# Retention: one small VectorE instruction with two tensor inputs becomes two with one tensor input each

## The chip, the core and the metric

The kernel runs on one core of a Trainium2 chip. A core has five engines that run their own instruction streams side by side and wait for each other by semaphores: TensorE (PE in the profile; its weight loads are PEld), VectorE (DVE), ScalarE (ACT), GpSimd (POOL) and SyncE (SP), which here issues most of the DMAs. The metric is the time of one execution on the device, in microseconds; lower is better.

## The reference

The program is one step of a two-layer decoder trunk on 1024 prompt tokens and 8 single-token sequences, all in fp32. Layer 0 is multi-scale retention, layer 1 a chunked gated MLP. What matters here is the end of the retention mixer: the output of each head, 512 wide, is normalised over its width, multiplied by a gain and by the SiLU of a gate, and projected.

```python
o = jnp.moveaxis(o, 0, 1).reshape(B, L, RET_HEADS, RET_DV)
mu = jnp.mean(o, -1, keepdims=True)
var = jnp.mean(jnp.square(o - mu), -1, keepdims=True)
o = ((o - mu) * lax.rsqrt(var + LN_EPS)).reshape(B, L, RET_VW) * gn_gain.astype(jnp.float32)
y = (jax.nn.silu(g.astype(jnp.float32)) * o).astype(x.dtype) @ w_out
```

## The kernel before

Every fp32 matmul is done as three: each operand is split into a high part (rounded) and a low part (the remainder), and high x high, high x low and low x high are summed in PSUM. The splits cost ScalarE a copy and VectorE or GpSimd a subtraction of two SBUF tensors.

The order of the work is the order of the code; nothing is rescheduled. The retention stage (some 580 to 770 us in the profile) is a loop of 16 rounds, n = 4h + c, over 4 heads and 4 chunks of 256 tokens each. A chunk has two row blocks of 128 tokens (`ib`). In round n the calls are, in this order:

- `r_stat(n - 1)`: VectorE takes the mean and variance of the two row blocks of the chunk before out of PSUM (`mv`, 128x2x2), adds epsilon (`rstn`), and GpSimd raises that to the power -1/2 (`rsrn`, line 254), which gives the reciprocal deviation.
- `r_pre(n + 1)`: PE transposes the keys of the next chunk (`kt`), VectorE makes their low part (`kd`); `r_split(n + 2)` then has GpSimd subtract for the low parts `qkl` and `vl` of the chunk after that, two instructions of 128x1024 on line 495, both inputs in SBUF; `r_on(n - 1)` comes next; then the scores `sc`, masked by VectorE to `p`, and their low part `phl` by GpSimd.
- `r_state(n)`: the running state `T`, and its split `sh` (ScalarE) and `sl` (VectorE, line 555, both inputs in SBUF).
- `r_inner(n)` and `r_cross(n)`: the output `o` in PSUM.
- `r_y(n - 1)`: PE transposes `on` (line 619), VectorE multiplies by gain and gate (`yT`, line 623: one input in PSUM, one in SBUF, and a column of gains). In the rounds with n mod 4 = 1, `r_cross(n)` comes ahead of it, in all others behind it. In round 0 of a head `r_cross` does nothing.

`r_on(n)` is the function that the change touches. It applies (o - mean) x deviation as one ScalarE pass per row block, with a scale and a bias per partition. The bias is -mean x reciprocal deviation, `nb`, 128x2, which VectorE makes from `mv` and `rsrn`. So `rsrn` (GpSimd) comes before `nb` (VectorE), that before `on` (ScalarE), and that before the transposes `y` (PE). The code issues the subtractions `qkl` and `vl` on GpSimd's queue directly behind `rsrn`, except in the last two rounds, where there is no chunk left to split; GpSimd has splits of the projection's weights (line 134) there.

Of the kernel before, what the change touches and what calls it, by code (L numbers as in the profile page):

```python
# [14 lines left out]
ALU = mybir.AluOpType  # L15
# [26 lines left out]
def retnet_gmlp_step(ctx: ExitStack, tc: tile.TileContext, a, o):  # L42
    nc = tc.nc
    act, dve, pool, pe, sp = nc.scalar, nc.vector, nc.gpsimd, nc.tensor, nc.sync
# [8 lines left out]
    def S(name, shape=(128, T), dt=F32):  # L53
        return big.tile(list(shape), dt, tag="s", name=name)
# [443 lines left out]
    def r_pre(n):  # L498
        if n >= NS:
            r_on(n - 2)  # L500
            return
        r = R[n]
        ps = PS(f"kt{n}")
        for jb in range(2):
            for d in range(2):
                pe.transpose(ps[:, jb * 256 + d * 128:jb * 256 + (d + 1) * 128],
                             r["qk"][:, 2 + d, jb * 128:(jb + 1) * 128], ident)
        kd = S(f"kd{n}", (128, 2, 512), F32R)
        act.copy(kd[:, 0, :], ps)
        dve.tensor_tensor(kd[:, 1, :], ps, f(kd[:, 0, :]), ALU.subtract)  # L510
        r["kd"] = kd
        if n:
            r_split(n + 1)
        r_on(n - 2)
        sc = PS(f"sc{n}")
        hh, ll = r["qkh"], r["qkl"]
        for jb in range(2):
            for d in range(2):
                ks = slice((2 + d) * CH + jb * 128, (2 + d) * CH + (jb + 1) * 128)
                qs = slice(d * CH + jb * 128, (d + 1) * CH)  # L520
                mm3(sc[:, jb * CH:CH + jb * 128], hh[:, ks], ll[:, ks], hh[:, qs], ll[:, qs], d == 0, d == 1)
        pt = S(f"p{n}", (128, 384))
        dve.tensor_tensor(pt, sc[:, :384], RC["mask"], ALU.mult)
        phl = S(f"phl{n}", (128, 2, 384), F32R)
        act.copy(phl[:, 0, :], pt)
        pool.tensor_tensor(phl[:, 1, :], pt, f(phl[:, 0, :]), ALU.subtract)
        r["p"] = phl
# [68 lines left out]
    def r_on(n):  # L596
        if n < 0:
            return
        r = R[n]
        rs = r["rs"]  # L600
        nb = small.tile([128, 2], F32, tag="nb", name=f"nb{n}")
        dve.scalar_tensor_tensor(nb, r["mv"][:, :, 0], -1.0, rs[:, 0:2], ALU.mult, ALU.mult)
        on = S(f"on{n}", (128, 2, DV))
        for ib in range(2):
            act.activation(on[:, ib, :], r["o"][ib], AF.Identity, bias=nb[:, ib:ib + 1], scale=rs[:, ib:ib + 1])
        r["on"] = on
# [326 lines left out]
    for n in range(NS):  # L933
# [19 lines left out]
        if n == NS - 1:  # L953
# [3 lines left out]
            outb.pre_load(1)  # L957
    r_stat(NS - 1)
    r_on(NS - 1)

    def r_last(q, n, tb):
# [589 lines left out]
```

## Time and profile before

| | |
|---|---|
| median of 3 runs | 1748.51 us (1746.86 to 1751.27) |
| the profiled execution | 1749.73 us, span 1748.0 us |
| PE busy, share of the span | 1692.2 us, 97% |
| VectorE, ScalarE, GpSimd busy | 900.0, 664.9, 407.5 us |
| mean granted TensorE clock | 0.987 of full |

The span is from the first to the last instruction of the program. Matmuls are pipelined, so a busy PE is not PE at its peak. [...] In a timeline row, the brackets at the end hold the idle time of the engine just before the instruction, and what ended it.

### The profile page before, as it was taken

How to read it: one execution, taken by the hardware profiler on the slowest of the kernel's cores; microseconds unless marked ns; L12 is line 12 of the kernel's file. 1: busy time of each engine (PE TensorE's matmuls, PEld its weight loads, DVE VectorE, ACT ScalarE, POOL GpSimd, SP SyncE). 2: the span in 40 equal slices, each digit the busy share in tenths (PEclk: the TensorE clock that was granted, in tenths of full speed). 3: DMA queues.
4: the chain of work that ended last, by engine and by line, in shares of the span. 5: the costliest groups of instructions: out<-in, count | busy, mean ns of one | idle time of the engine just before them, and what ended most of it. 6: DMA issues, size and time to landing. Idle time of an engine off the chain costs nothing. (4 is left out here: it accounts for less than half of the span.)

```text
span 1748.0 us, 25438 instructions
## 1 busy us (share of the span) xinstructions
PE 1692.2 (97%) x10304; PEld 1511.5 (86%) x10304; DVE 900.0 (51%) x1446; ACT 664.9 (38%) x1043; POOL 407.5 (23%) x331
## 2 busy tenths in 40 slices
PE   9999999999999999999999999997899999999996
PEld 8898897979999887877778999996889999977775
DVE  7134453633331577753359574564465555543347
ACT  4122424234332454431205343344556666731102
POOL 4122231411110666531107100011111111231103
PEclk9999999999999999999999999998999999999998
DMA  7135555555532544341102312263655666692206
GB/s 266 72 122 191 183 204 187 212 165 209 217 145 93 197 157 157 133 181 49 49 25 110 110 73 97 84 178 78 152 147 151 157 164 157 152 324 89 82 1 171
DMA packets 103174, 248.76 MB, mean 142 GB/s; under 512 B 9264, under 2 KB 37824, under 8 KB 103056
## 3 DMA queue, kind: packets, MB, share of 16 engines
q1 hardware_dynamic: 92736, 222.78, 36.5%
q0 software_dynamic: 10112, 24.15, 7.8%
q8 instruction: 81, 1.33, 0.3%
q14 instruction: 37, 0.30, 0.0%
q10 hardware_dynamic: 208, 0.20, 0.0%
HBM read 152.83 MB, written 69.93 MB: 127 GB/s over the span
## 5 line engine op out<-in xcount | busy, mean ns | idle before, releaser
L63 PE MATMUL fm<-xl,wh 128*128 128x344 f32 x768 | 246.6, 321 | 1.2 <-DVE xl L301 0.8
L63 PE MATMUL fm<-xh,wh 128*128 128x344 f32 x768 | 246.4, 321 | 1.3 <-ACT xh L300 1.3
L63 PE MATMUL fm<-xh,wl 128*128 128x344 f32 x768 | 246.1, 320 | 0.0
L63 PE MATMUL op<-wh,yh 128*128 128x512 f32 x512 | 202.4, 395 | 0.0
L63 PE MATMUL op<-wl,yh 128*128 128x512 f32 x512 | 201.7, 394 | 0.0
L63 PE MATMUL op<-wh,yl 128*128 128x512 f32 x512 | 201.7, 394 | 0.0
L63 PEld LDWEIGHTS fm<-xh,wh 128*128 128x128 f32 x768 | 144.9, 189 | 5.6 <-ACT xh L300 2.0
L63 PEld LDWEIGHTS fm<-xl,wh 128*128 128x128 f32 x768 | 144.7, 188 | 3.0 <-DVE xl L301 1.3
L63 PEld LDWEIGHTS fm<-xh,wl 128*128 128x128 f32 x768 | 144.7, 188 | 0.0
L130 ACT CAST wh<-wr 128x1024 fp32r<-128x1024 f32 x83 | 86.0, 1047 | 143.0 <-PE pd L63 58.9
L665 DVE TENSOR_TENSOR pre<-pre,op 128x512 f32<-128x512 f32 x96 | 65.7, 684 | 141.4 <-PE op L63 141.4
L134 DVE TENSOR_TENSOR wl<-wr,wh 128x1024 fp32r<-128x1024 f32 x77 | 107.6, 1403 | 46.2 <-ACT wh L130 28.6
L412 DVE SCALAR_TENSOR_TENSOR dw<-s,qd_dec,dw 128x512 f32<-128x512 f32 x32 | 40.0, 1251 | 170.1 <-ACT dw L411 170.1
L63 PEld LDWEIGHTS op<-wh,yh 128*128 128x128 f32 x512 | 96.1, 188 | 23.8
L63 PEld LDWEIGHTS op<-wh,yl 128*128 128x128 f32 x512 | 96.1, 188 | 22.7
L63 PEld LDWEIGHTS op<-wl,yh 128*128 128x128 f32 x512 | 96.2, 188 | 22.2
L63 PE MATMUL tm<-wl,xh 128*128 128x512 f32 x256 | 101.1, 395 | 0.0
L63 PE MATMUL tm<-wh,xl 128*128 128x512 f32 x256 | 100.9, 394 | 0.0
L63 PE MATMUL tm<-wh,xh 128*128 128x512 f32 x256 | 100.9, 394 | 0.0
L420 POOL TENSOR_TENSOR dhl<-dw,dhl 128x512 fp32r<-128x512 f32 x32 | 43.3, 1353 | 242.3 <-ACT dhl L419 234.4
L355 ACT ACTIVATE v<-tm,gneg 128x512 f32<-128x512 f32 x32 | 22.0, 689 | 202.3 <-PE tm L63 184.6
L1171 POOL DMA_DIRECT2D w_p<-wr x32 | 28.6, 895 | 295.8 <-PE tm38a L63 169.6
(829 smaller groups left out, 4262.4 us busy)
## 6 DMA issues: line engine op xcount, KB each, us to landing
wr<-in_w SPq DMA_DIRECT2D x127, 512.0 KB
s<-in_state SPq DMA_DIRECT2D x32, 512.0 KB
out_rs<-s SPq DMA_DIRECT2D x32, 512.0 KB
y_s<-yy SPq DMA_DIRECT2D x17, 512.0 KB
qk_s<-ro SPq DMA_DIRECT2D x16, 512.0 KB
v_s<-v SPq DMA_DIRECT2D x16, 512.0 KB
vbc<-vd_s SPq DMA_DIRECT2D x16, 512.0 KB
g_s<-g SPq DMA_DIRECT2D x16, 512.0 KB
```

The costliest lines, as they stand in the source:

```text
L63: pe.matmul(out, lhs, rhs, start=start, stop=stop, skip_group_check=skip)
L130: act.copy(t, src)
L134: eng.tensor_tensor(t, src, f(W[p][half][0]), ALU.subtract)
L355: act.activation(t[:, i % 2, :], ps, AF.Copy, scale=gneg[:, 2 * h + i % 2:2 * h + i % 2 + 1])
L412: dve.scalar_tensor_tensor(w[:, 0, :], s[:, 0, :], qd_dec[:, h, 0, b:b + 1], w[:, 1, :], ALU.mult, ALU.add)
L420: pool.tensor_tensor(hl[:, 1, :], w, f(hl[:, 0, :]), ALU.subtract)
L665: dve.tensor_tensor(dst, dst, ps, ALU.add)
L1171: pool.dma_start(self.op[k][1], src, accum_op=ALU.add)
```

## The change

Line 602 made both columns of `nb` with one SCALAR_TENSOR_TENSOR, whose two tensor inputs are the means and the reciprocal deviations, both in SBUF. Now there is a loop over the two row blocks with one TENSOR_SCALAR each: its tensor input is the column of means (128x1), and it is multiplied by the constant -1 and by the column of reciprocal deviations, which is read as a per-partition scalar.

```diff
         nb = small.tile([128, 2], F32, tag="nb", name=f"nb{n}")
-        dve.scalar_tensor_tensor(nb, r["mv"][:, :, 0], -1.0, rs[:, 0:2], ALU.mult, ALU.mult)
+        for ib in range(2):
+            dve.tensor_scalar(nb[:, ib:ib + 1], r["mv"][:, ib, 0:1], -1.0, rs[:, ib:ib + 1], ALU.mult, ALU.mult)
         on = S(f"on{n}", (128, 2, DV))
```

VectorE's queue in round 1, where `nb` of chunk 0 is made, before (line, operation, out<-in, size, and the semaphores that the instruction waits for; the numbers behind names are buffers):

```order
L510 TENSOR_TENSOR kd_4929<-kt_4924,kd_4929 128x512 [waits Activation_49]
L602 SCALAR_TENSOR_TENSOR nb_4940<-mv_4915,rsrn_4921 128x2 [waits Pool_49]
L523 TENSOR_TENSOR p_4958<-sc_4945,mask 128x384 [waits PE_49]
L549 SCALAR_TENSOR_TENSOR T_4977<-T_4890,st_0_4963 128x512 [waits PE_49]
L549 SCALAR_TENSOR_TENSOR T_4977<-T_4890,st_1_4970 128x512 [waits PE_49]
L555 SCALAR_TENSOR_TENSOR sl_4981<-T_4977,sh_4980 128x1024 [waits Activation_49]
```

The same place with the change:

```order
L510 TENSOR_TENSOR kd_4929<-kt_4924,kd_4929 128x512 [waits Activation_49]
L603 TENSOR_SCALAR nb_4940<-mv_4915,rsrn_4921 128x1 [waits Pool_49]
L603 TENSOR_SCALAR nb_4940<-mv_4915,rsrn_4921 128x1
L523 TENSOR_TENSOR p_4959<-sc_4946,mask 128x384 [waits PE_49]
L549 SCALAR_TENSOR_TENSOR T_4978<-T_4890,st_0_4964 128x512 [waits PE_49]
L549 SCALAR_TENSOR_TENSOR T_4978<-T_4890,st_1_4971 128x512 [waits PE_49]
L555 SCALAR_TENSOR_TENSOR sl_4982<-T_4978,sh_4981 128x1024 [waits Activation_49]
```

One instruction became two in the same place, the first of which waits for GpSimd as the old one did; no other instruction of VectorE changes its place.

ScalarE's queue in the same round, before:

```order
L494 CAST vh_4936<-vv_4909 128x1024 [waits DMAHW7_49]
L605 ACTIVATE on_4942<-o_0_4897,nb_4940,rsrn_4921 128x512 [waits DVE_49]
L605 ACTIVATE on_4942<-o_1_4898,nb_4940,rsrn_4921 128x512
L525 CAST phl_4960<-p_4958 128x384 [waits DVE_49]
L554 ACTIVATE sh_4980<-T_4977 128x1024 [waits DVE_49]
```

The same with the change:

```order
L494 CAST vh_4936<-vv_4909 128x1024 [waits DMAHW7_49]
L606 ACTIVATE on_4943<-o_0_4897,nb_4940,rsrn_4921 128x512 [waits DVE_49]
L606 ACTIVATE on_4943<-o_1_4898,nb_4940,rsrn_4921 128x512 [waits DVE_49]
L525 CAST phl_4961<-p_4959 128x384 [waits DVE_49]
L554 ACTIVATE sh_4981<-T_4978 128x1024 [waits DVE_49]
```

The second half of `on` now has a wait of its own on VectorE.

## Rows read from the trace of the kernel before

**Rows 1.** The page, part 1: busy us, share of the span, instructions.
```profile
PE 1692.2 (97%) x10304; PEld 1511.5 (86%) x10304; DVE 900.0 (51%) x1446; ACT 664.9 (38%) x1043; POOL 407.5 (23%) x331
```

**Rows 2.** PE's waits, 580 to 770 us: total us, times, longest.
```profile
PE y L619 <- ACT on L605: 10.3, 12, 2.4
```

**Rows 3.** Windows, PE: stretch, length, busy (instructions), granted clock, DMA share, GB/s.
```profile
601.31:616.48 15.17, 12.41 (x60) 0.89 0.06 19
611.40:614.80 3.40, 3.40 (x12) 0.50 0.00 0
616.48:626.83 10.35, 10.35 (x58) 1.00 0.27 82
...
644.75:657.64 12.89, 10.78 (x59) 1.00 0.20 70
668.50:676.90 8.40, 8.01 (x47) 1.00 0.97 312
687.62:702.40 14.78, 12.15 (x59) 0.88 0.33 107
696.80:700.20 3.40, 3.08 (x11) 0.50 0.00 0
```

**Rows 4.** Line 602: grouped (busy us, mean ns | idle before); then ns min/median/max.
```profile
L602 DVE SCALAR_TENSOR_TENSOR nb<-mv,rsrn 128x2 f32<-128x2 f32 x16 | 22.3, 1393 | 5.1 <-POOL rsrn L254 5.1
...
L602 DVE SCALAR_TENSOR_TENSOR nb<-mv,rsrn x16: 160/2331/2391, 596.6 to 757.9; 128x2 f32<-128x2 f32 x16
```

**Rows 5.** Timeline, 607 to 612 us, round 2: start us, us, engine, instruction.
```profile
607.28 2.38 POOL L495 TENSOR_TENSOR qkl<-qk,qkh 128x1024 fp32r<-128x1024 f32 x1
607.34 2.33 DVE L602 SCALAR_TENSOR_TENSOR nb<-mv,rsrn 128x2 f32<-128x2 f32 x1 [0.20 <-POOL rsrn L254]
...
609.60 2.36 POOL L495 TENSOR_TENSOR vl<-vv,vh 128x1024 fp32r<-128x1024 f32 x1
609.76 1.45 ACT L605 ACTIVATE on<-o,nb,rsrn 128x512 f32<-128x512 f32 x2 [5.33 <-DVE nb L602]
...
610.60 0.33 PE L619 MATMUL y<-ident,on 128*128 128x128 f32 x1 [2.42 <-ACT on L605]
...
611.92 1.00 POOL L526 TENSOR_TENSOR phl<-p,phl 128x384 fp32r<-128x384 f32 x1
```

**Rows 6.** Timeline, 735 to 738 us, round 14, without splits on line 495.
```profile
735.74 0.16 DVE L602 SCALAR_TENSOR_TENSOR nb<-mv,rsrn 128x2 f32<-128x2 f32 x1 [0.21 <-POOL rsrn L254]
735.82 0.56 DVE L523 TENSOR_TENSOR p<-sc,mask 128x384 f32<-128x384 f32 x1
736.00 1.45 ACT L605 ACTIVATE on<-o,nb,rsrn 128x512 f32<-128x512 f32 x2 [4.08 <-DVE nb L602]
...
737.37 0.90 PE L619 MATMUL y<-ident,on 128*128 128x128 f32 x6
```

**Rows 7.** Timeline, 944 to 947 us, the projection behind retention.
```profile
944.43 2.39 POOL L713 TENSOR_TENSOR pre<-pre,lnb 128x1024 f32<-128x1024 f32 x1 [1.26 <-ACT pre L705]
...
945.75 0.15 DVE L251 TENSOR_SCALAR rstl<-lmv 128x1 f32<-128x1 f32 x1
```

**Rows 8.** Timeline, 1529 to 1534 us, in layer 1.
```profile
1528.90 2.41 POOL L134 TENSOR_TENSOR wl<-wr,wh 128x1024 fp32r<-128x1024 f32 x1
1529.01 2.33 DVE L1380 CAST y1d<-ydt 128x8 fp32r<-128x8 f32 x1
...
1531.37 2.28 DVE L1381 TENSOR_TENSOR y1d<-ydt,y1d 128x8 fp32r<-128x8 f32 x1
```

**Rows 9.** Timeline, 730 to 733 us.
```profile
730.62 3.40 POOL L134 TENSOR_TENSOR wl<-wr,wh 128x1024 fp32r<-128x1024 f32 x1
...
731.67 1.65 DVE L623 SCALAR_TENSOR_TENSOR yT<-y,gng,gg 128x256 f32<-128x256 f32 x4
```

**Rows 10.** Timeline, 675 to 680 us, round 9.
```profile
677.42 1.45 DVE L555 SCALAR_TENSOR_TENSOR sl<-T,sh 128x1024 fp32r<-128x1024 f32 x1 [3.41 <-ACT sh L554]
677.75 2.00 POOL L526 TENSOR_TENSOR phl<-p,phl 128x384 fp32r<-128x384 f32 x1
```

## The prediction

> **What bounds the kernel now.** I read the page's busy shares first: TensorE (PE) is busy for 1692.2 of 1748.0 us [rows 1], so a change counts only where PE stands still or runs slowly. Second, PE's waits in the retention stage, 580 to 770 us: one line holds nearly all of it, the transposes of `on` waiting for ScalarE, 10.3 us in 12 waits, the longest 2.4 [rows 2]. Third, the stage cut into its rounds [rows 3]. A round of one kind (c = 1, 2 or 3 of a head) takes 10.35 us where nothing stops it; three others take 15.17, 12.89 and 14.78. [...]
>
> Fourth, the instruction that the change replaces. `nb` is 128x2, yet its 16 instances take 22.3 us, 1393 ns on average, from 160 to 2391 [rows 4]. Instances of 2.35 and of 0.16 us give 22.3 with nine long and seven short ones. The timeline shows what a long one is [rows 5]: GpSimd starts `qkl`, a subtraction with both inputs in SBUF, at 607.28; `nb` starts at 607.34 and ends at 609.67, when `qkl` ends at 609.66. It is a hold and not work. Behind it ScalarE had been idle for 5.33 us, starts `on` at 609.76, and PE starts `y` at 610.60 after 2.42 us of waiting; with the wait for the second half of `on` the round has 15.17 - 12.41 = 2.76 us of PE idle [rows 3]. In the last head the same round has no subtraction behind the power: `nb` takes 0.16 us, `on` starts 0.26 us after `nb`, and PE transposes without a wait [rows 6].
>
> **The change, part by part.** Removed: 16 instances, nine of about 2.35 us and seven of 0.16. Added: 32 TENSOR_SCALAR of 128x1. The trace has that operation and size elsewhere: 0.15 us at 945.75 [rows 7]. Behind a short `nb` the next VectorE instruction starts 0.08 us after it started (735.82 after 735.74 [rows 6]), so a second small one costs 0.08 to 0.16 and I take 0.25 for the pair. ScalarE's second half now waits for the second one alone, which is done 0.8 us before the first half of `on` is, so that wait is free.
>
> The question is whether TENSOR_SCALAR is held too. The rows say no, in two halves. At 945.75 a 128x1 TENSOR_SCALAR began 1.3 us into a GpSimd addition of 2.39 us with two SBUF inputs, and took 0.15 us [rows 7]. That one had a constant where the new one has a column of `rs` from SBUF. For that operand, `yT` has one tensor from PSUM, one from SBUF and a column from SBUF: four in a row took 1.65 us inside a GpSimd subtraction of 3.40 us [rows 9]; these are free of a hold, so a column does not bring one. What the trace lacks is both in one instruction. Bounds for a pair: 0.25 us (not held) and 4.6 us (both held, one after the other, as the 2.33 and 2.28 us at 1529.01 and 1531.37 [rows 8]). I take 0.25, since the nearest row in operation and size is not held.
>
> A held `nb` then ends 2.35 - 0.25 = 2.1 us sooner, nine times. Seven unheld ones end about 0.1 us later; of those, most stand behind ScalarE's casts, where 0.1 us does not show, so I count nothing.
>
> What PE gets of it:
> - Its waits for `on`, 10.3 us [rows 2]. One, in the round 668.50 to 676.90, follows an unheld `nb` (span less busy 8.40 - 8.01 = 0.4 us [rows 3]) and stays. That leaves 9.9 us. The three waits in c = 2 rounds (span less busy: 2.76; 12.89 - 10.78 = 2.1; 14.78 - 12.15 = 2.6 [rows 3]) are as long as the gain of 2.1 or longer, so 0.7 + 0 + 0.5 = 1.2 us would be left over by that alone. But the round before also lets VectorE finish earlier, since its `nb` is held too. I leave 0.8: gain 9.1 us.
> - The clock. With waits of at most 0.7 us in place of 2.4, I expect both stretches at 0.50 to run at 1.00. A stretch of 3.4 us at half speed holds 1.7 us of full-speed work, so each returns 1.7: gain 3.4 us. This is the 0.89 and 0.88 in the mean clock of the two rounds.
> - Restarts. Round 644.75 is 12.89 - 10.35 = 2.54 us over its undisturbed like, of which 2.11 is wait; round 601.31 is 4.82 over, of which 2.76 + 1.7 = 4.46. So some 0.4 us a stopped round goes into refilling PE; three such: 1.0 us.
>
> Sum: 9.1 + 3.4 + 1.0 = 13.5 us. What is late next? VectorE's `sl`, the other instruction here with two SBUF inputs. It now asks during `vl`, 2.1 us sooner, and is held until that ends; at 677.42 it was, then ran ahead of GpSimd's `phl`, which was drawn out to 2.00 us from 1.00 in the round of [rows 5] [rows 10]. `phl` is read a round later, so that is covered. If `phl` goes first instead, VectorE keeps its old finishing time, the 1.2 us above stay whole and a wait of 0.7 us recurs. Loads do not become the bound: they are issued as tiles come free, which moves with PE.
>
> The rest of the program has PE as its bound too, so what the stage gains reaches the end. The profiled execution took 1749.73 us (span 1748.0), 1.2 above the median of the runs, 1748.51. 1748.51 - 13.5 = 1735.0.
>
> [...] At 1529.01 a cast of 128x8, one tensor input, is held for 2.33 us behind a GpSimd subtraction [rows 8], so a single input is no safeguard. [...]
>
> **Rivals.**
> - Slower: the pair is held, twice in a row. The first part ends with `qkl`, as `nb` does now; the second then starts inside `vl`, which follows at 609.60 [rows 5], and is held for another 2.3 us, as the pair at 1529.01 was. `on` comes 2.3 us later. In six rounds PE already waits on it with `vl` behind (the three above, and three with waits of 0.2 to 0.4 in what is left of the 10.3), so 6 x 2.3 = 14 us, and one to four more clock stretches at 1.7 each: 16 to 21, say 1767. It decides as soon as the second instruction meets a GpSimd subtraction. Against it: the row at 945.75. Chance 0.07.
> - No effect: only the first is held, the second slips through between `qkl` and `vl`. 1748.5 give or take 1. `vl` starts before `nb` ends [rows 5], so there is hardly a gap. Chance 0.05.
> - Part of it given back: the hold goes, but `sl` and `phl` take turns the other way, or the clock falls elsewhere. 13.5 less 1 to 2 of leftover waits, less 3.4 of clock, less their restarts: a gain of 5 to 10, about 1740. For it: later stages have their own stretches at 0.50 which a shift by 13 us may move by one or two. Chance 0.18, of which 0.02 with under 5.2 us.
> - The forecast: all three terms, a gain of 11 to 17: 1732 to 1738. Chance 0.70.
>
> **How the numbers follow.** A measurement of this kernel tells 0.3% (5.2 us) from no change. Faster by more: 0.70 + 0.16 = 0.86. Within: 0.05 + 0.02 = 0.07. Slower: 0.07. The time is the forecast's, 1735. The range leaves out the two held cases (0.12) and a little of the small gains: below, every microsecond of the four rounds' excess plus one moved clock stretch elsewhere (18 us); above, the gain of waits without clock and with leftovers (6 us): 1730 to 1742.5.
>
> **What would show it.** Right: all 32 TENSOR_SCALAR at about 0.15 us with `qkl` running; ScalarE's idle time ended by `nb` down by some 2 us a held round; PE's waits for `on` down from 10.3 to 1 or 2 us; no clock of 0.50 between 600 and 735; the three long rounds at 10.4 to 11. Wrong: a TENSOR_SCALAR of 2.3 us, above all the second of a pair; PE's wait for `on` replaced by one for `phl` or `sl`; the stage shorter and the end not.

## The result, and the profile after

The changed kernel takes 1733.07 us (median of 4 runs, 1732.42 to 1735.48) where the one before takes 1748.34 (median of 4): ratio 0.9913, 95% interval 0.9896 to 0.9930, so 12 to 18 us faster. In a later set of runs it was 1733.88 us, ratio 0.9916, 0.9903 to 0.9930. The forecast was 1735.

The timeline of the changed kernel in round 2, the stretch that answers to [rows 5] (here and below, rows that don't bear on the reading are left out of timelines):

```profile
605.84 0.70 POOL L254 TENSOR_TENSOR rsrn<-rstn,mhalf 128x2 f32<-128x2 f32 x1 [2.39 <-DVE rstn L253]
606.51 2.42 POOL L495 TENSOR_TENSOR qkl<-qk,qkh 128x1024 fp32r<-128x1024 f32 x1
606.57 0.33 DVE L603 TENSOR_SCALAR nb<-mv,rsrn 128x1 f32<-128x1 f32 x2 [0.20 <-POOL rsrn L254]
...
606.88 1.45 ACT L606 ACTIVATE on<-o,nb,rsrn 128x512 f32<-128x512 f32 x2 [2.92 <-DVE nb L603]
...
607.72 0.33 PE L620 MATMUL y<-ident,on 128*128 128x128 f32 x1
...
608.38 0.98 PE L620 MATMUL y<-ident,on 128*128 128x128 f32 x7 [0.34 <-ACT on L606]
...
609.75 2.60 DVE L555 SCALAR_TENSOR_TENSOR sl<-T,sh 128x1024 fp32r<-128x1024 f32 x1 [1.19 <-ACT sh L554]
611.23 1.99 POOL L526 TENSOR_TENSOR phl<-p,phl 128x384 fp32r<-128x384 f32 x1
```

GpSimd's `qkl` starts at 606.51, and the pair runs beside it in 0.33 us. PE's wait of 2.42 us is gone; 0.34 for the second half of `on` is left. `sl` is now the instruction that is held (2.60 us; the shortest of its 12 instances here takes 1.23), it then runs ahead of `phl`, which takes 1.99 us, and PE waits for neither.

All 32 instances of the new instruction (ns min/median/max), and the waits of PE in the stage, 580 to 770 us:

```profile
L603 DVE TENSOR_SCALAR nb<-mv,rsrn x32: 201/210/217, 596.8 to 744.0; 128x1 f32<-128x1 f32 x32
```

```profile
PE y L620 <- ACT on L606: 0.3, 1, 0.3
PE sc L63 <- POOL qkl L495: 0.3, 1, 0.3
```

None is held, at most 217 ns each, though 11 of the 16 pairs run inside a GpSimd subtraction (9 instances, of 2.33 to 2.39 us, were held before). PE waits 0.3 us in the place of the 10.3 of [rows 2]. The rounds of the changed kernel, stretch, length, PE busy, clock, which answer to [rows 3]:

```profile
600.84:611.99 11.15, 10.80 (x60) 1.00 0.13 46
611.99:622.34 10.35, 10.35 (x59) 1.00 0.18 58
640.29:650.95 10.66, 10.56 (x59) 1.00 0.25 85
661.29:669.09 7.80, 7.79 (x47) 1.00 0.99 322
679.40:690.09 10.69, 10.57 (x59) 1.00 0.45 149
```

The three long rounds went from 15.17, 12.89 and 14.78 to 11.15, 10.66 and 10.69 us, at clock 1.00 throughout. The first projection matmul starts at 737.57 us, before at 751.65: the stage gives 14.1 us. What lies behind it is the same program in both. From that matmul to the end, in the kernel before, after, and in the second profile of the changed kernel:

```profile
751.65:1748.02 996.37, 954.97 (x6225) 0.98 0.42 121
```

```profile
737.57:1730.71 993.14, 951.42 (x6225) 0.99 0.42 122
```

```profile
737.49:1732.83 995.34, 955.22 (x6225) 0.98 0.41 122
```

The 3.2 us by which the first profile was shorter there came back in part in the second. Over the profiles of the eight experiments that leave this part alone it takes from 992.0 to 999.0 us, so the 3.2 us lie within its scatter and are not claimed for the change. At least a part of the scatter is the clock: between 760 and 1700 us the kernel before has 27.3 us at 0.50, the first profile of the changed kernel 17.1, the second 27.3 again.

### The profile page after: what moved, and what is told of

Its sections match the earlier page's. It is cut to its first block, busy times and chain, and to the rows that moved or that the text cites. A ratio compares the mean times of both kernels' runs of the same rounds, so it can differ in the third digit from the quotient of the medians.

```text
span 1730.7 us, 25453 instructions
## 1 busy us (share of the span) xinstructions
PE 1685.0 (97%) x10304; PEld 1506.6 (87%) x10304; DVE 891.3 (52%) x1462; ACT 665.0 (38%) x1043; POOL 413.5 (24%) x331
```

## The experiments

The theory: a VectorE instruction that reads two SBUF tensors is held while GpSimd runs a subtraction that reads SBUF; `nb` was such an instruction on the path to PE. Rivals: the old form is slow in itself; the split into two, or the size, is what counts and not the number of inputs; the gain comes from elsewhere in the stream. Each kernel was timed beside the one before on the same chip (1748.4 to 1749.2 us).

**1. Split, but two inputs each.**

```diff
-        dve.scalar_tensor_tensor(nb, r["mv"][:, :, 0], -1.0, rs[:, 0:2], ALU.mult, ALU.mult)
+        for ib in range(2):
+            dve.scalar_tensor_tensor(nb[:, ib:ib + 1], r["mv"][:, ib, 0:1], -1.0, rs[:, ib:ib + 1], ALU.mult, ALU.mult)
```

> nb split in two as in the change, but each half a SCALAR_TENSOR_TENSOR with both columns as tensor inputs (128x1). Theory (what holds is the second SBUF input): the first half is held by qkl, the second by vl, some 4.6 us together where it was 2.35; this is the rival of the prediction that ends on the other side: 16 to 21 us slower than before, 1764 to 1769 us. Rival (it is the size of one element a row, or the split, that frees it): as with the change, 1733 us.

Measured: 1752.24 us, ratio 1.0018 (1.0007 to 1.0029). Its timeline in round 2, and all instances:

```profile
607.03 2.37 POOL L495 TENSOR_TENSOR qkl<-qk,qkh 128x1024 fp32r<-128x1024 f32 x1
607.10 2.39 DVE L603 SCALAR_TENSOR_TENSOR nb<-mv,rsrn 128x1 f32<-128x1 f32 x2 [0.20 <-POOL rsrn L254]
609.36 2.36 POOL L495 TENSOR_TENSOR vl<-vv,vh 128x1024 fp32r<-128x1024 f32 x1
...
610.34 0.33 PE L620 MATMUL y<-ident,on 128*128 128x128 f32 x1 [2.41 <-ACT on L606]
```

```profile
L603 DVE SCALAR_TENSOR_TENSOR nb<-mv,rsrn x32: 144/156/2387, 596.4 to 760.0; 128x1 f32<-128x1 f32 x32
```

Size, number and place are those of the change, and so is ScalarE's separate wait for the second half; only the operation differs, and with it the kind of the second operand. The gain is gone. So neither the split nor the size of one element frees `nb` by itself. It is not the operation's name either: in [rows 9] the same one, with one of its tensors in PSUM, is not held (four inside the subtraction take 0.47 us each, the median of all 64). But my price for a second hold was wrong: both together took 2.39 us and not 4.6. The second instruction, queued right behind the first without a wait, gets in as `qkl` ends and `vl` starts (609.34 and 609.36). The pair at 1529.01 [rows 8] was held twice (2.33 and 2.28 us), and there the second waits for the first's result; that this difference is the cause was not tried.

**2. One input, two elements a row, made beside the power.**

```diff
+        ng = small.tile([128, 2], F32, tag="ng", name=f"ng{n}")
+        dve.tensor_scalar(ng, r["mv"][:, :, 0], -1.0, None, ALU.mult)
+        for ib in range(2):
+            dve.tensor_scalar(nb[:, ib:ib + 1], ng[:, ib:ib + 1], rs[:, ib:ib + 1], None, ALU.mult)
```

> Each instruction has one tensor input, but the first is 128x2: the means are negated in one TENSOR_SCALAR of 128x2 with a constant, then multiplied by the deviations in two of 128x1. Theory A (one tensor input is never held): as with the change, plus 0.15 us a chunk: 1733 to 1735 us, all 48 instructions at about 0.2 us. Theory B (one input is held as well when its size along the row is even, as the 128x8 cast was; one element is not): the 128x2 one is held 2.3 us in nine or more chunks, the two behind it run free: 1748 to 1752 us.

Measured: 1731.94 us, ratio 0.9913 (0.9893 to 0.9933). It reads like theory A, but the test was a poor one, as its timeline in round 1 shows:

```profile
595.84 0.73 POOL L254 TENSOR_TENSOR rsrn<-rstn,mhalf 128x2 f32<-128x2 f32 x1 [0.82 <-DVE rstn L253]
596.28 0.16 DVE L603 TENSOR_SCALAR ng<-mv 128x2 f32<-128x2 f32 x1
596.50 2.44 POOL L495 TENSOR_TENSOR qkl<-qk,qkh 128x1024 fp32r<-128x1024 f32 x1
596.61 0.34 DVE L605 TENSOR_SCALAR nb<-ng,rsrn 128x1 f32<-128x1 f32 x2 [0.17 <-POOL rsrn L254]
```

`ng` needs the means alone, so it was done before `qkl` started and never met it. It says nothing about a hold by a subtraction. It did start inside GpSimd's power `rsrn`, which reads SBUF too, in 14 of 16 chunks, and that did not hold it (0.16 us at 596.28, with the power running from 595.84 to 596.57).

**3. The same, but waiting for the power.**

```diff
+        ng = small.tile([128, 2], F32, tag="ng", name=f"ng{n}")
+        dve.tensor_scalar(ng, rs[:, 0:2], -1.0, None, ALU.mult)
+        for ib in range(2):
+            dve.tensor_scalar(nb[:, ib:ib + 1], ng[:, ib:ib + 1], r["mv"][:, ib, 0:1], None, ALU.mult)
```

> Like the experiment with one tensor input and 128x2, but now the 128x2 instruction negates the deviations, so it can only start when GpSimd's power is done, that is with qkl: it meets the subtraction as the old nb did. Theory A (one tensor input in SBUF is not held): 0.16 us each, 1733 to 1735 us. Theory B (one input of even size along the row is held, as the 128x8 cast was at 1529 us): 2.3 us in nine or more of 16, PE waits 10 us for on: 1748 to 1752 us.

Measured: 1750.73 us, ratio 1.0020 (1.0009 to 1.0030). Round 2, and all instances of both instructions (ns min/median/max):

```profile
607.01 2.39 POOL L495 TENSOR_TENSOR qkl<-qk,qkh 128x1024 fp32r<-128x1024 f32 x1
607.08 2.35 DVE L603 TENSOR_SCALAR ng<-rsrn 128x2 f32<-128x2 f32 x1 [0.20 <-POOL rsrn L254]
609.36 2.36 POOL L495 TENSOR_TENSOR vl<-vv,vh 128x1024 fp32r<-128x1024 f32 x1
609.46 0.33 DVE L605 TENSOR_SCALAR nb<-ng,mv 128x1 f32<-128x1 f32 x2
```

```profile
L603 DVE TENSOR_SCALAR ng<-rsrn x16: 169/2350/2403, 596.3 to 760.4; 128x2 f32<-128x2 f32 x16
...
L605 DVE TENSOR_SCALAR nb<-ng,mv x32: 202/210/216, 598.7 to 760.7; 128x1 f32<-128x1 f32 x32
```

Theory B holds. One tensor input is not enough: at 128x2 the same operation is held for 2.35 us, and at 128x1, 0.1 us after `vl` has started, it runs in 0.33 for two. The change gains by both of its properties together, one tensor input and one element a row. `ng` also reads another tensor than `nb` does and has a constant in place of the column; but the 128x8 cast of [rows 8], on yet another tensor, is held too, and the 128x1 instruction of [rows 7], with a constant, is not, so the width is what is left. Whether an odd width above one is held was not tried. At 128x1 a column as the second operand does not bring a hold: at most 217 ns in all 32 instances of the change, at most 216 in the 32 here.

**4. Without the subtraction beside it.** The old `nb`, but `r_on` called ahead of `r_split`; and the new one in the same order.

```diff
-        if n:
-            r_split(n + 1)
         r_on(n - 2)
+        if n:
+            r_split(n + 1)
         sc = PS(f"sc{n}")
```

> The old instruction (128x2, two tensor inputs), but r_on is called ahead of r_split, so that ScalarE's casts for the split, and with them GpSimd's qkl and vl, can only start behind nb and on. Theory (the hold, and nothing about the instruction itself, cost the time): nb takes 0.16 us in 15 of 16 chunks (in round 15 a subtraction of line 134 still runs), PE's waits for on go with it, but for the 1.6 us of that round: 14.1 - 2 = 12 us faster, 1736 us, if qkl and vl, now some 2 us later, stay hidden. Rival (the old form is slower in itself, or the gain came from ScalarE's separate wait): 1748 us.

> Both: the two TENSOR_SCALAR, and r_on ahead of r_split. Theory: nothing is left to gain by it but the 0.3 to 0.7 us that PE still waits for on: 1733 us, give or take 2; slower by up to 5 us if the later splits make PE wait for qkl (it waited 0.3 us once).

Measured: 1744.62 us with the old `nb` (ratio 0.9981, 0.9969 to 0.9994) and 1744.39 with the new (0.9976, 0.9962 to 0.9989). The old instruction and PE's waits in the first of them:

```profile
L602 DVE SCALAR_TENSOR_TENSOR nb<-mv,rsrn x16: 160/160/2340, 596.3 to 753.9; 128x2 f32<-128x2 f32 x16
```

```profile
PE y L619 <- ACT on L605: 4.0, 7, 1.9
PE sc L63 <- POOL qkl L495: 3.1, 4, 1.8
```

As the theory has it, the old form takes 0.16 us where no subtraction runs (15 of 16), and then it makes no difference which form is used. The times of both missed: the splits come so late that PE waits 3.1 and, with the new form, 5.5 us for `qkl`. The waits for `on` did not go either (4.0 and 3.5 us); the longest, 1.9 and 2.0 us, is no hold of `nb`: GpSimd's power itself comes late there, behind a split of the weights on line 134. And the stage still has two stretches at clock 0.50 with the old form and one with the new; the round from 630.45 to 644.45 us with the old form, in which PE waits 1.8 us for `qkl`, runs at a mean of 0.88. The hold was taken away and waits for GpSimd's later work came in its place.

**5. One part of the chunks.** The new pair only in the four chunks with c = 1, whose `nb` stands ahead of the three longest waits (and of one that was not held); then its complement.

```diff
-        dve.scalar_tensor_tensor(nb, r["mv"][:, :, 0], -1.0, rs[:, 0:2], ALU.mult, ALU.mult)
+        if n % NCH == 1:
+            for ib in range(2):
+                dve.tensor_scalar(nb[:, ib:ib + 1], r["mv"][:, ib, 0:1], -1.0, rs[:, ib:ib + 1], ALU.mult, ALU.mult)
+        else:
+            dve.scalar_tensor_tensor(nb, r["mv"][:, :, 0], -1.0, rs[:, 0:2], ALU.mult, ALU.mult)
```

> The two TENSOR_SCALAR in the four chunks with c = 1 alone, the old instruction in the other twelve. Theory (a two-input nb is held by GpSimd's subtraction, and the end moves where PE waits for it): three of the nine held instances go, those behind the three long rounds. Their waits of 2.76, 2.11 and 2.63 us fall by 2.0 each (6 us, some 1.2 stay, since VectorE is not sooner in the round before), both clock stretches return 3.4, restarts 1.0: about 10.5 us, 1738 us. Rival (the gain comes from the instruction stream as a whole, spread over all 16 instances): 4/16 of 15.3, 1744.5 us.

> The complement: the old instruction in the four chunks with c = 1, the two TENSOR_SCALAR in the other twelve. Theory: the three long waits stay, but start from a VectorE that is about 1 us sooner, so 2.4 becomes some 1.5; the 1.6 us of the last round and 0.8 in small waits go: 2.4 + 2.9 = 5.3 us, and another 3.4 if waits of 1.5 us no longer bring the clock down: 1743 or 1739.5 us. Rival (spread evenly): 12/16 of 15.3, 1737 us.

Measured: 1747.87 us for c = 1 alone (ratio 0.9991, 0.9980 to 1.0002, which does not exclude no change) and 1741.64 for the others (0.9960, 0.9947 to 0.9974). The complement came out between my two figures: its three long waits are 2.1, 0.6 and 1.8 us, without a stretch at clock 0.50, and PE has a new wait of 1.4 us for `yl`. The first was a plain miss, 1.4 us in place of 10.5. Its rounds, its old and new instructions of `nb` (busy us, mean ns), and PE's waits for `on`:

```profile
601.00:612.43 11.43, 10.79 (x60) 1.00 0.07 24
612.43:624.36 11.93, 10.78 (x59) 1.00 0.13 42
624.36:632.35 7.99, 7.76 (x46) 1.00 1.00 318
632.35:643.71 11.36, 10.82 (x59) 1.00 0.84 288
```

```profile
L606 DVE SCALAR_TENSOR_TENSOR nb<-mv,rsrn 128x2 f32<-128x2 f32 x12 | 19.5, 1623 | 4.3 <-POOL rsrn L254 4.3
...
L604 DVE TENSOR_SCALAR nb<-mv,rsrn 128x1 f32<-128x1 f32 x8 | 1.3, 210 | 0.9 <-POOL rsrn L254 0.9
```

```profile
PE y L623 <- ACT on L609: 9.7, 24, 1.3
```

The round of 15.17 us became 11.43, but the next one, 10.35 before, became 11.93. Of the twelve old instances eight are held (8 x 2.35 + 4 x 0.16 = 19.4); of the same twelve, six were before. The waits for `on` are shorter and twice as many, 9.7 us in the place of 10.3. Both stretches at 0.50 are gone (3.4 us), but in each stopped round PE is busy for some 0.4 us more (10.79 against 10.35), and more rounds are stopped. From 580 us to the first projection matmul PE is busy for 160.42 us, where before it was 161.15 with the clock's 3.4 in it: 2.7 more. So 0.6 + 3.4 - 2.7 leaves little of the gain. A new held instance is that of chunk 2; here, and ahead of it the same instance of the kernel before:

```profile
617.59 1.05 ACT L494 CAST qkh<-qk 128x1024 fp32r<-128x1024 f32 x1
618.65 0.16 DVE L602 SCALAR_TENSOR_TENSOR nb<-mv,rsrn 128x2 f32<-128x2 f32 x1 [0.23 <-POOL rsrn L254]
618.72 2.40 POOL L495 TENSOR_TENSOR qkl<-qk,qkh 128x1024 fp32r<-128x1024 f32 x1
```

```profile
616.80 2.40 POOL L495 TENSOR_TENSOR qkl<-qk,qkh 128x1024 fp32r<-128x1024 f32 x1
616.87 2.35 DVE L606 SCALAR_TENSOR_TENSOR nb<-mv,rsrn 128x2 f32<-128x2 f32 x1 [0.27 <-POOL rsrn L254]
```

Before, this `nb` started 0.07 us ahead of `qkl` and got through; with a shorter round in front, `qkl` is first by 0.07 and holds it. Both come behind the same power, but `qkl` also needs ScalarE's cast `qkh`: before, that ended at 618.64, the power at 618.62; here it ended at 614.60, long ahead of the power. So which is first changes with little. Freeing one hold lets the next round run into one. Alone, the two parts are worth 1.4 and 7.6 us, together 15: the waits of single rounds don't add up, and the gain is there only when no round is held.

**6. The same cure elsewhere.** The changed kernel once more, and with it a version in which the three small instructions of `s_y` for feature block 14, held behind GpSimd's splits in layer 1 (1.65, 2.32 and 2.28 us in the changed kernel), go to GpSimd's own queue.

```diff
-        dve.tensor_tensor(t.rearrange("p (i t) -> p i t", i=2), mdT[:, fb, :].rearrange("p (i t) -> p i t", i=2), ugd,
+        eng = pool if fb == 14 else dve
+        eng.tensor_tensor(t.rearrange("p (i t) -> p i t", i=2), mdT[:, fb, :].rearrange("p (i t) -> p i t", i=2), ugd,
...
-        dve.tensor_copy(y1d[:, fb, 0:8], t)
-        dve.tensor_tensor(y1d[:, fb, 8:16], t, f(y1d[:, fb, 0:8]), ALU.subtract)
+        eng.tensor_copy(y1d[:, fb, 0:8], t)
+        eng.tensor_tensor(y1d[:, fb, 8:16], t, f(y1d[:, fb, 0:8]), ALU.subtract)
```

> The changed kernel once more, beside the two below, for a second profile of the program behind retention: the first had 993.1 us from the first projection matmul to the end where the kernel before had 996.4, though not an instruction differs there. Theory (that part only scatters from run to run): 1733 us, and from 992 to 999 us behind retention, as in the six experiments. Rival (the shift by 14 us always saves 3 us there): 993 again.

> The change, and the same cure at the one other place where a held VectorE instruction ends a PE wait: in layer 1 the last but one s_y has three small instructions (ydt, y1d, y1d) held for 1.6, 2.3 and 2.3 us behind GpSimd's splits, and fm55a waits 1.98 us behind them. They go to GpSimd's own queue in that one call. Theory: PE's wait of 1.98 us goes, and now and then a clock stretch with it (four of seven traces have one there): 2 to 3 us faster than the change, 1731 us. Rival (GpSimd's splits come later by the three and PE waits for those instead): no gain, 1733 us or more.

Measured: 1733.88 us for the change (ratio 0.9916, 0.9903 to 0.9930) and 1731.68 with the cure (0.9912, 0.9898 to 0.9926). The wait that it was to remove, in the changed kernel:

```profile
PE fm55a L63 <- DVE s L1194: 2.0, 1, 2.0
```

With the cure no wait of PE is left between 1490 and 1550 us. The median is 2.2 us lower, as expected, but the intervals overlap almost wholly: whether this version is the faster one is not shown.

## Why the prediction was right

- The hold: right. `nb` ended with `qkl`, and it was the operands and not the work; experiment 1 (same size and number, two inputs: held) against the change (not held), and experiment 4 (old form, nothing beside it: 0.16 us).
- TENSOR_SCALAR of 128x1 is not held: right, and the column operand, the half that no row had shown together, did not matter. At 128x2 a single tensor input would have been held (2.35 us in experiment 3).
- The pair's 0.25 us: it took 0.33; one instruction with a column takes 0.21 us where the one with a constant took 0.15 [rows 7].
- PE's waits, 9.1 us: PE's idle time ahead of `y` fell from 10.3 to 0.7 us in sum (0.3 in the wait shown above, the rest in shorter gaps), 9.6. The longest of the three long rounds, 11.15 us, is a little above the 11 named. The 0.4 us that was to stay, in the round of 8.40 us, went too (7.80, PE busy 7.79). The clock, 3.4: both stretches at 0.50 are gone; PE was busy for only 3.08 us of the second [rows 3], so 3.2 would have been the better figure. Half the speed at 0.50 was my estimate: in the first, matmuls of 128x512 start 0.43 us apart (613.57, 614.00), right behind it 0.23 (614.85, 615.08). That the waits bring the clock down, which the 3.4 rests on, was my estimate too, from two places; no run shows it as a rule (last section), only that here both stretches went with the waits. Restarts, 1.0: the 14.1 us of the stage less 9.6 and 3.4 leave 1.1, and PE's busy time from 580 us to the first projection matmul fell by 4.6 (161.15 to 156.59), which less the clock's 3.2 to 3.4 leaves 1.2 to 1.4; that PE is being refilled in it was not shown. The sum was 13.5, and 14.1 was measured for the stage. That the median moved by 15.3 is within the interval.
- What is late next: right. `sl` is held (2.60 us in round 2) and delays `phl` (1.99 us in the place of 1.00 [rows 5]), and neither reaches PE.
- The slower rival's mechanism was wrong in its price: a second hold of 2.3 us, which made its 1767 us, did not come in experiment 1, which had what it supposed. That pair, of which only the first was held, cost 3 us over the kernel before. The rival called no effect, in which the second slips through, was the one to fear.
- Where my picture was too simple: I counted each round's wait by itself, and left the seven unheld instances unheld. In the changed kernel eleven pairs meet a subtraction and not nine, so the old form would have been held twice more there; experiment 5 shows that with part of the change the waits move to other rounds. The sum was right because the change takes them all.

## What to carry to other kernels

A small VectorE instruction that takes fifteen times as long as its like (2.35 against 0.16 us) was held here, not slow: look at what GpSimd runs beside such a one, and whether the two start from the same event. The form that was free here has one tensor input and one element a row, with the other operand as a column; one input alone did not do at two elements, nor one element with two inputs. Judge such a cure on all instances together: with a part of them freed, the loop ran into the next hold.

## What the runs showed of the hardware that I had not expected

A VectorE instruction queued right behind a held one was not held by GpSimd's next subtraction, though the two begin together: in the eight such places of experiment 1 it started within 0.03 us of `vl` (598.64 against 598.62 in one, mostly just ahead) and took 0.15 us. GpSimd's spans overlap there (`qkl` lasts until 598.70), so which of the two was really first is open.

And the clock is no sure consequence of a wait of PE. Both waits of 2.4 us in the kernel before went with 3.4 us at 0.50, of which one began 0.8 us after the wait had ended and the other some 0.2 us before, but only three of the six of 2.3 to 2.5 us in experiments 1 and 3. Of waits of 1.8 to 2.1 us, three of the four in experiment 4 did, and neither of the two in the complement of experiment 5, whose rounds of 13.24 and 12.96 us ran at 1.00. Behind the retention stage of the changed kernel a wait of 2.0 us that ended at 1159.53 went with a stretch at 0.50, and one of 2.6 us that ended at 1199.06 did not. What brings the clock down is not shown.
